# A one-core decoder step in split fp32: how a norm's squares are summed, where the last pair's low weight is made, who issues the sample rows, and a root written with one product less

## The chip, the cores and the metric

The program runs on one core of one Trainium2 chip. The metric is device time in microseconds (us) of one execution, the median of several runs. Five engines work side by side and wait for each other by semaphores: TensorE (PE in the profile; PEld is its weight load), VectorE (DVE), ScalarE (ACT), GpSimd (POOL) and SyncE (SP), which here only issues DMAs. Every engine takes its instructions in the order in which the program lists them.

## The reference

One layer of a hybrid decoder, for a prompt of 512 tokens and eight samples of four tokens each (544 columns in all), all in float32. With the names of the reference:

```
h = RMSNorm_pre(x);  [x_r | q | k | v | g] = h @ W_in
m = (sigmoid(g_A) * (lru(x_r) @ W_A) + sigmoid(g_B) * (attn(q,k,v) @ W_B)) @ W_out
x = x + RMSNorm_post(m)
u = RMSNorm_pre2(x) @ W_up ; u = causal depthwise conv (width 3) over positions
x = x + RMSNorm_post2((gelu(u_gate) * u_val) @ W_down)
```

where an RMSNorm is

```
y = x32 * lax.rsqrt(jnp.mean(x32 * x32, axis=-1, keepdims=True) + EPS) * g
```

The new rows of x and the recurrent, window and convolution states are the outputs. The width of x is 1024, of the feed-forward part 4096 (8192 columns up, gate and value).

## The kernel before

**Layout.** Activations lie transposed: 128 features on the partitions, tokens along the free axis. A [1024, 544] activation is eight chunks; a chunk is worked on in two halves of tokens, of 272 columns each after the mixer. A float32 product is made of three fast ones: each weight and each operand is split into a high part (a copy in the fast format, by ScalarE) and a low part (raw minus high, by VectorE), and TensorE adds high times high, high times low and low times high. A "product" in this text is 12 such matmuls: four 128-row chunks by three. The weight tiles `wh_...` and `wl_...` are the high and low parts. TensorE's order is written by hand, and so is the order of ScalarE, VectorE and GpSimd around the changes; the raw weights are loaded by SyncE several units ahead into five rotating buffers.

**The norm between mixer and feed-forward** (`norm_chain`, from L1233) runs once for each half of the tokens, as a generator whose pieces are slipped between TensorE's products. For the second half (a = 1) it does this, two chunks to a group g: VectorE scales the mixer's output (`mt`, L1258); the residual is added to give `x1` (names `x_0` to `x_7` in the trace), for even chunks on GpSimd (L1260) and for odd ones on VectorE (L1262); ScalarE squares each chunk into `sq_x` (L1266), chunk 0 straight into the sum `accx`. The other seven squares have to be added into `accx`. Two of these additions are done by DMAs that GpSimd issues (L1270): the squares of chunks 2 and 3 are accumulated into that of chunk 1, in memory, one DMA after the other since both write the same tile. VectorE adds 4, 5, 6, the collected chunk 1, and 7 (L1273). TensorE then sums over the partitions (`pst_f`), ScalarE and VectorE make the reciprocal root (`nst_f`) and a diagonal (`dg_f`), TensorE spreads it (`rep_f`), and VectorE writes the normed second half (`h2t`, split into `b12H` and so on).

Meanwhile TensorE works through early products on the first half: `pq` of columns 0, 32, 1, 33, 2, 34, 3, 35, each in two halves of the weight rows (`wh_e_0` or `wh_e_1`, split at L1465 on ScalarE, and `wl_e` at L168 on VectorE). ScalarE's and VectorE's instructions for these weights stand in the same queues as those of the norm.

**The feed-forward part** goes over 32 pairs (gate and value columns). A pair's up-projection, three-tap convolution (`tap`: the first on ScalarE, L1559; the other two on VectorE, tile `uc`), gelu, product `z` and split (`fH`, `fL`) are spread over later slots by `later(k, ...)`: k slots from now. `slot(k, lag)` closes a slot: it emits what is due in it, then the weights ahead (`consumed`, `ahead`: high parts by `do_high`, low parts lag units behind by `do_low`). Products with W_down (`pmdn`) go into three rotating PSUM banks (`PM`, L134), and VectorE adds each into `ft` (L1717, helper L174). For the last pair, 31, the chain is written out at L1683 to L1688.

**The end** (from L1925): tokens 256 to 511 and the sample rows go out transposed (`yo`, copied by ScalarE at L1811, issued by SyncE at L1812); of tokens 128 to 255 the two halves `xtok` are scaled by the reciprocal root `r` (L1895) and issued at L1896. The root is ScalarE's square root, a reciprocal, and one Newton step on VectorE (L1940 to L1944), all on 128x1 tiles `nst_t`.

Of the kernel before, what the change touches and what calls it, by code (L numbers as in the profile page):

```python
# [14 lines left out]
ALU = mybir.AluOpType  # L15
AX = mybir.AxisListType

P = 128
D = 1024
# [104 lines left out]
def hawk_step(ctx, tc, I, O):  # L124
    nc = tc.nc
# [47 lines left out]
    def add(out, a, b):  # L173
        dve.tensor_tensor(out=out, in0=a, in1=b, op=ALU.add)  # L174
# [1058 lines left out]
    def norm_chain(a, acc):  # L1233
# [8 lines left out]
        with tc.high_priority(offset=HP):  # L1242
            rep = spread(dg, n, f"m{a}")
            acc2 = T(f"accx{a}")
            sq = {}

            def x1_(c):
                return x1[c][:, lo:hi]

            for c in range(0 if a else 8):  # L1250
                m_ = mt[c][:, lo:hi]
                stt(m_, m_, pv[:, G_POST + c:G_POST + c + 1], rep[:, :n], ALU.mult, ALU.mult)
                pool.tensor_tensor(out=x1_(c), in0=x1_(c), in1=m_, op=ALU.add)
                sq_sum(acc2, x1_(c), n, c == 0, f"x{a}_{c}")
            for g in range(6 if a else 0):
                for c in range(2 * g, 2 * g + 2) if g < 4 else ():
                    m_ = mt[c][:, lo:hi]
                    stt(m_, m_, pv[:, G_POST + c:G_POST + c + 1], rep[:, :n], ALU.mult, ALU.mult)  # L1258
                    if c % 2 == 0:
                        pool.tensor_tensor(out=x1_(c), in0=x1_(c), in1=m_, op=ALU.add)  # L1260
                if g < 4:
                    add(x1_(c), x1_(c), m_)  # L1262
                for c in range(2 * g - 3, 2 * g - 1) if 1 <= g < 6 else ():
                    if 0 <= c < 8:
                        sq[c] = acc2 if c == 0 else T(f"sq_x{a}_{c}")
                        act.activation(sq[c][:, :n], x1_(c), AF.Square)  # L1266
                        if c == 0 and n % P:
                            pool.memset(acc2[:, n:n + P - n % P], 0.0)
                        if c in (2, 3):
                            pool.dma_start(out=sq[1][:, :n], in_=sq[c][:, :n], accum_op=ALU.add)  # L1270
                for c in ((), (), (), (), (4,), (5, 6, 1, 7))[g]:
                    if c:
                        add(acc2[:, :n], acc2[:, :n], sq[c][:, :n])  # L1273
                yield 0.5
        yield NORM_TICKS[a]
        with tc.high_priority(offset=HP):
# [364 lines left out]
    def pair(p_, nm):  # L1641

        jv, jg = p_, 32 + p_
        ps, e = pst.setdefault(p_, {}), e_.setdefault(p_, {})
        bank = {"a11": "x", "a12": "z", "p2": "x", "p3": "y", "p1": "x", "p4": "w" if p_ in apart else "x",
                "a22": "y"}[nm]
        start = bank not in ps
        if start:
            ps[bank] = PX(f"pu{bank}_{p_}")
        product(ps[bank], usplit["s", p_, nm], XOF[nm], start, nm in ("a12", "p4", "a22") or bank == "x" and nm == "p1" and p_ in apart)  # L1650
        z = ps[bank][:, :HN]

        def taken(nm_):

            e[nm_] = EP(f"{nm_}_{p_}")
            act.copy(e[nm_], z)  # L1656

        def u4_c22():
            taken("u4")
            ug = utile(jg)  # L1660
            for o, y in zip(halves2(ug, ps["y"]), halves2(ug, e["u4"])):
                sub(o[0], o[1], y[1])

        def c11():
            add(utile(jv)[:, 2:2 + HN], e["e1"], z)

        def c12():
            if p_ in apart:
                for o, y in zip(halves2(ut[jv], z), halves2(ut[jv], e["u4"])):
                    add(o[0], y[1], o[1])  # L1670
            else:
                for o in halves2(ut[jv], z):
                    act.copy(*o)
            states(jg if p_ < 31 else jv)

        def c21():
            sub(ut[jg][:, 2:2 + HN], z, e["u2"])
            states(jv if p_ < 31 else jg)

        if nm in ("a11", "a12", "p2", "p1", "p4", "a22"):  # L1680
            f = {"a11": lambda: taken("e1"), "a12": c11, "p2": lambda: taken("u2"), "p1": u4_c22, "p4": c12, "a22": c21}[nm]
            result(f)
        if p_ == 31 and nm in ("a22", "p4"):  # L1683
            j = jg if nm == "a22" else jv
            chain = [(1, tap, j, 0), (1, tap, j, 1), (2, tap, j, 2)]
            chain += [(2, glu, p_, 0)] if j == jg else [(2, glu, p_, 1), (3, glu, p_, 2), (3, glu, p_, 3)]
            for k, f, *args in chain:
                later(k, f, *args)  # L1688
        elif nm == "a22":
            for k, f, *args in ((1, tap, jv, 0), (2, tap, jv, 1), (2, tap, jg, 0), (3, tap, jv, 2), (4, tap, jg, 1),  # L1690
                                (5, tap, jg, 2), (6, glu, p_, 0), (7, glu, p_, 1), (8, glu, p_, 2), (9, glu, p_, 3)):
                later(k + 3 if k >= 8 and p_ % CH == CH - 1 else k, f, *args)
# [77 lines left out]
    for i, x in enumerate(plan):  # L1770
        more[0] = min(4, max(0, i - len(plan) + LASTS))
        if x[0] == "s":
            pair(*x[1:])
            slot()
        elif x[0] == "q":
            plain(*x)
            slot(x[3])
        else:
            _, q, c, a = x
            down(q, c, a, down_done(q, c))  # L1780
            slot(a)
        if i == len(plan) - 8:
            start_at(now[0] + 1, x1_again())
            start_at(now[0] + 3, ffn_states())
# [18 lines left out]
    def rows_t(i):  # L1803
        t0, nn, _ = TOK[i]
        dst = yp[t0:t0 + nn, :] if i < 4 else ys
        o = RAW(f"yo{i}")
        for kk in range(2):
            px = PX(f"pyo{i}_{kk}")
            for j in range(4):
                pe.transpose(px[:nn, j * P:(j + 1) * P], ft[4 * kk + j][:, t0:t0 + nn], ident)  # L1810
            act.copy(o[:nn, kk * 512:(kk + 1) * 512], px[:nn, :])  # L1811
        return lambda: nc.sync.dma_start(out=dst, in_=o[:nn, :])  # L1812

    sq7 = T("sq7")
    frow, fgs = {}, {}
# [108 lines left out]
        tokens_out(0, r0, z)()  # L1924
    order_.enter_context(tc.manual_schedule(engines={nc.sync.engine}))  # L1925
    fgs[1, 1] = T("fg1_1")[:, 0:512]
    st = SM("nst_t1", [P, 4], "nst_t")
    v, r, s_, b_ = (st[:, z:z + 1] for z in range(4))
    yo = [rows_t(2)]
    o = ends(0)  # L1930
    ends_square(0, o)
    ends_gain(0, o)
    add(b_, ssq[:, 1, 0:1], ssq[:, 1, 1:2])
    dve.tensor_scalar(b_, b_, 1.0 / D, EPS, ALU.mult, ALU.add)
    o = ends(1)
    ends_square(1, o)
    act.activation(s_, ssq[:, 1, 2:3], AF.Sqrt, scale=1.0 / D, bias=b_)
    ends_gain(1, o)
    yo += [rows_t(i) for i in (3, 4)]
    stt(v, ssq[:, 1, 2:3], 1.0 / D, b_, ALU.mult, ALU.add)  # L1940
    dve.reciprocal(r, s_)
    mul(s_, r, r)
    stt(s_, s_, -0.5, v, ALU.mult, ALU.mult)
    stt(r, s_, 1.5, r, ALU.add, ALU.mult)  # L1944
    xo = [tokens_out(1, r, z) for z in range(2)]
    for f in yo[:2] + xo[:1] + yo[2:] + xo[1:]:
        f()
    flush()
    order_.close()
# [32 lines left out]
```

## Time and profile before

| | |
|---|---|
| median of 3 runs | 997.18 us (996.15, 997.18, 998.26) |
| the profiled execution's own time | 998.1 us |
| its span, from first to last instruction | 996.3 us |
| mean granted clock of TensorE | 0.993 |
| PE busy | 985.0 us (99%) |
| DVE busy | 745.5 us (75%) |
| ACT busy | 557.8 us (56%) |
| POOL busy | 162.1 us (16%) |

The 1.8 us between 996.3 and 998.1 lie outside the recorded span. In the profile a row of the timeline gives start and length in us, the engine, the line of the program, the operation with output and inputs, the shape, how many instructions are merged ("x2"), and in brackets how long the engine had been idle before and what released it. A row of the waits gives waiter, its line, releaser, total us, times, longest. A row of a table by windows gives the stretch, its length, the busy time of PE, PEld, DVE, ACT (and POOL) with the number of instructions, TensorE's granted clock (1.00 is full speed), the DMA engines' busy share and GB/s.

### The profile page before, as it was taken

Reading aid. Unit: us, or ns where it says so; the run is one execution under the profiler, and the core shown is the slowest. Engines: PE = TensorE matmul, PEld = TensorE weight load, DVE = VectorE, ACT = ScalarE, POOL = GpSimd, SP = SyncE. Lnnn points to the kernel's source line nnn. Section 1 sums busy time; section 2 is a strip of 40 time slices with the busy share of each in tenths; the row PEclk is TensorE's granted clock in tenths of the full one; section 3 lists DMA queues with packets and bytes.
Section 4 is the critical chain, followed back from the end, with each engine's and each line's share of the span. In section 5 each row is a group of like instructions: output and inputs, shape, how many; then the busy total and the mean of one; then the engine's idle time right before and its main releaser. Section 6 shows DMA issues by size and latency. Waiting matters only on the chain.

```text
span 996.3 us, 20129 instructions
## 1 busy us (share of the span) xinstructions
PE 985.0 (99%) x7780; PEld 976.5 (98%) x7780; DVE 745.5 (75%) x1608; ACT 557.8 (56%) x1356; POOL 162.1 (16%) x273
## 2 busy tenths in 40 slices
PE   9999999999999999989999999999999999999997
PEld 8999999999999999989999999999999999999996
DVE  6677678767858555678787788888888888888765
ACT  6545334468476425545776655555655555556652
POOL 2162000002406341210001010101010101011004
PEclk9999999999999999998999999999999999999999
DMA  7674222333223535135147767676767677768612
GB/s 209 198 246 146 86 64 86 107 97 95 87 70 99 175 112 171 44 120 171 48 117 155 164 150 168 152 167 152 167 152 167 153 165 154 164 151 199 196 46 90
DMA packets 211399, 135.90 MB, mean 136 GB/s; under 512 B 8997, under 2 KB 197421, under 8 KB 211272
## 3 DMA queue, kind: packets, MB, share of 16 engines
q1 hardware_dynamic: 199032, 112.72, 39.6%
q0 software_dynamic: 12208, 19.87, 11.9%
q10 hardware_dynamic: 64, 2.04, 0.6%
q8 instruction: 61, 1.00, 0.4%
q14 instruction: 34, 0.28, 0.1%
HBM read 111.78 MB, written 11.37 MB: 124 GB/s over the span
## 4 chain that ended last, share of the span: by engine, by line
PE 96%; ACT 1%; DVE 1%; issue 1%; POOL 0%; DMA 0%; DVEq 0%; ACTq 0%; POOLq 0%
PE pmin L165 22%; PE pmdn L165 17%; PE pux L1528 16%; PE puy L1528 8%; PE pq L1528 7%; PE pmout L165 5%; PE pmao L165 5%; PE pmlo L165 5%; PE puz L1528 4%; PE pg L165 1%; PE psc L165 1%; PE pvp L165 1%; PE ptok L165 1%; PE pt L819 1%; PE ps_warm L165 0%
## 5 line engine op out<-in xcount | busy, mean ns | idle before, releaser
L165 PE MATMUL pmin<-hH,wh_in 128*128 128x256 f32 (+1 forms) x568 | 164.7, 292 | 0.0
L165 PE MATMUL pmin<-hL,wh_in 128*128 128x256 f32 (+1 forms) x568 | 162.3, 288 | 0.0
L165 PE MATMUL pmin<-hH,wl_in 128*128 128x256 f32 (+1 forms) x568 | 159.0, 288 | 0.0
L165 PE MATMUL pmdn<-fH,wh_dn 128*128 128x256 f32 (+1 forms) x448 | 129.3, 289 | 0.2 <-DVE ft L174 0.2
L165 PE MATMUL pmdn<-fH,wl_dn 128*128 128x256 f32 (+1 forms) x448 | 129.2, 288 | 0.0
L165 PE MATMUL pmdn<-fL,wh_dn 128*128 128x256 f32 (+1 forms) x448 | 128.8, 287 | 0.0
L177 DVE SCALAR_TENSOR_TENSOR uc<-u,fv,uc 128x560 f32<-128x560 f32 x128 | 101.9, 796 | 13.3 <-ACT uc L1559 13.2
L165 PEld LDWEIGHTS pmin<-hH,wh_in 128*128 128x128 f32 x568 | 107.2, 189 | 1.5 <-issue 1.2
L165 PEld LDWEIGHTS pmin<-hL,wh_in 128*128 128x128 f32 x568 | 107.3, 189 | 0.1
L165 PEld LDWEIGHTS pmin<-hH,wl_in 128*128 128x128 f32 x568 | 104.7, 188 | 0.2 <-issue 0.2
L165 PEld LDWEIGHTS pmdn<-fH,wh_dn 128*128 128x128 f32 x448 | 84.3, 188 | 0.6 <-issue 0.6
L165 PEld LDWEIGHTS pmdn<-fL,wh_dn 128*128 128x128 f32 x448 | 84.4, 188 | 0.0
L165 PEld LDWEIGHTS pmdn<-fH,wl_dn 128*128 128x128 f32 x448 | 84.4, 188 | 0.0
L1656 ACT COPY u<-pux 128x272 f32<-128x272 f32 x52 | 20.1, 386 | 86.3 <-PE pux L1528 86.3
L168 DVE TENSOR_TENSOR u<-puy,u 128x240 f32<-128x240 f32 (+2 forms) x78 | 24.6, 344 | 50.2 <-PE puy L1528 33.2
L283 ACT ACTIVATE wh_in<-raw_in 128x512 fp32r<-128x512 f32 x70 | 42.8, 627 | 31.6 <-issue 17.8
L174 DVE TENSOR_TENSOR ft<-ft,pmdn 128x256 f32<-128x256 f32 (+1 forms) x104 | 45.1, 435 | 17.2 <-PE pmdn L165 16.9
L290 DVE TENSOR_TENSOR wl_in<-raw_in,wh_in 128x512 fp32r<-128x512 f32 x70 | 48.0, 696 | 1.0 <-ACT wh_in L283 1.0
L1559 ACT ACTIVATE uc<-u,fv 128x560 f32<-128x560 f32 x64 | 48.3, 756 | 0.0
L1454 POOL DMA_DIRECT2D raw_up_s<-raw_up_s x26 | 22.4, 863 | 100.3 <-DMA raw_up_s<-raw_up__7493 4.9
L168 DVE TENSOR_TENSOR wl_dn<-raw_dn,wh_dn 128x512 fp32r<-128x512 f32 x56 | 38.3, 683 | 0.0
L776 ACT ACTIVATE s<-s,st 128x256 f32<-128x256 f32 (+1 forms) x32 | 15.2, 475 | 40.7 <-DVE st L773 23.1
(777 smaller groups left out, 3413.3 us busy)
## 6 DMA issues: line engine op xcount, KB each, us to landing
raw_in<-in_w_in_dram SPq DMA_DIRECT2D x35, 512.0 KB
raw_dn<-in_w_down_dram SPq DMA_DIRECT2D x56, 256.0 KB
raw_up_s<-in_w_up_dram SPq DMA_DIRECT2D x25, 512.0 KB
raw_up_s<-raw_up_s POOLq DMA_DIRECT2D x26, 256.0 KB, 5.2
raw_ao<-in_w_attn_o_dram SPq DMA_DIRECT2D x8, 512.0 KB
raw_lo<-in_w_lru_o_dram SPq DMA_DIRECT2D x8, 512.0 KB
raw_out<-in_w_out_dram SPq DMA_DIRECT2D x8, 512.0 KB
xdram<-xn POOLq DMA_DIRECT2D x8, 272.0 KB, 11.4
```

Of the source, the lines that this page charges most:

```text
L165: pe.matmul(out, l, r, start=start, stop=stop)
L168: dve.tensor_tensor(out=out, in0=a, in1=b, op=ALU.subtract)
L174: dve.tensor_tensor(out=out, in0=a, in1=b, op=ALU.add)
L177: dve.scalar_tensor_tensor(out=out, in0=a, scalar=s_, in1=b, op0=op0, op1=op1)
L283: act.activation(hl[0], raw, AF.Copy)
L290: (eng or dve).tensor_tensor(out=hl[1], in0=raw, in1=f32(hl[0]), op=ALU.subtract)
L776: act.activation(s3[:, j, :], s3[:, j, :], AF.Exp, bias=ng[:, j:j + 1], accum_out=sm[:, j:j + 1])
L819: pe.transpose(pt[:, (2 * ch + j) * P:(2 * ch + j + 1) * P], s3[:, j, ch * P:(ch + 1) * P], ident)
L1454: pool.dma_start(out=w["p4"], in_=w["p2"], accum_op=ALU.add)
L1528: pe.matmul(ps[:, :HN], w, x, start=start and k == 0 and i == 0, stop=stop and k == 3 and i == 2, skip_group_check=True)
L1559: act.activation(yt[j][:, 0:FLATU], u[:, 0:FLATU], AF.Copy, scale=fv[:, j:j + 1])
L1656: act.copy(e[nm_], z)
```

## The change

Four edits, which touch different places.

1. In the second half's norm, the two accumulating DMAs of GpSimd are gone. VectorE adds all seven squares, in two blocks: 1, 2, 3 in group 4, and 4, 5, 6, 7 in group 5.
2. In the last pair, the second tap of the value column moves one slot later, and the slot that closes the pair makes its low weight part with lag 0 instead of 1.
3. The sample rows' output DMA is issued by ScalarE's queue instead of SyncE's.
4. In the last root, minus one half of the mean square is prepared before the last sum arrives (`h_`), and `r * r * v` is one instruction in place of two. The tile is one column wider and has buffers of its own.

```diff
@@ norm_chain
                         act.activation(sq[c][:, :n], x1_(c), AF.Square)
                         if c == 0 and n % P:
                             pool.memset(acc2[:, n:n + P - n % P], 0.0)
-                        if c in (2, 3):
-                            pool.dma_start(out=sq[1][:, :n], in_=sq[c][:, :n], accum_op=ALU.add)
-                for c in ((), (), (), (), (4,), (5, 6, 1, 7))[g]:
-                    if c:
-                        add(acc2[:, :n], acc2[:, :n], sq[c][:, :n])
+                for c in ((), (), (), (), (1, 2, 3), (4, 5, 6, 7))[g]:
+                    add(acc2[:, :n], acc2[:, :n], sq[c][:, :n])
                 yield 0.5
@@ pair
-            chain = [(1, tap, j, 0), (1, tap, j, 1), (2, tap, j, 2)]
+            chain = [(1, tap, j, 0), (1 if j == jg else 2, tap, j, 1), (2, tap, j, 2)]
@@ the loop over the plan
             pair(*x[1:])
-            slot()
+            slot(1, int(x[1:] != (31, ENDS[-1])))
@@ rows_t
-        return lambda: nc.sync.dma_start(out=dst, in_=o[:nn, :])
+        return lambda q=nc.sync: q.dma_start(out=dst, in_=o[:nn, :])
@@ the end
-    st = SM("nst_t1", [P, 4], "nst_t")
-    v, r, s_, b_ = (st[:, z:z + 1] for z in range(4))
+    st = SM("nst_t1", [P, 5], "nst_t1")
+    v, r, s_, b_, h_ = (st[:, z:z + 1] for z in range(5))
...
     dve.tensor_scalar(b_, b_, 1.0 / D, EPS, ALU.mult, ALU.add)
+    dve.tensor_scalar(h_, b_, -0.5, 0.0, ALU.mult, ALU.add)
...
-    stt(v, ssq[:, 1, 2:3], 1.0 / D, b_, ALU.mult, ALU.add)
+    stt(v, ssq[:, 1, 2:3], -0.5 / D, h_, ALU.mult, ALU.add)
     dve.reciprocal(r, s_)
-    mul(s_, r, r)
-    stt(s_, s_, -0.5, v, ALU.mult, ALU.mult)
+    stt(s_, r, r, v, ALU.mult, ALU.mult)
     stt(r, s_, 1.5, r, ALU.add, ALU.mult)
     xo = [tokens_out(1, r, z) for z in range(2)]
-    for f in yo[:2] + xo[:1] + yo[2:] + xo[1:]:
+    yo[2](act)
+    for f in yo[:2] + xo:
         f()
```

TensorE's order is the same in both programs. The three places below are where the other engines' orders differ.

On GpSimd, in the second half's norm (`x_0` to `x_6` are the even residual chunks, `mt` the scaled mixer output, `sq_x_1` the tile that collects squares):

```order
 L1260 TENSOR_TENSOR x_0_4621<-x_0_4621,mt_5223 128x272
 L1260 TENSOR_TENSOR x_2_4623<-x_2_4623,mt_5225 128x272
-L1270 DMA sq_x_1_6016<-sq_x_2_6018 128x272
 L1260 TENSOR_TENSOR x_4_4625<-x_4_4625,mt_5227 128x272
-L1270 DMA sq_x_1_6016<-sq_x_3_6044 128x272
 L1260 TENSOR_TENSOR x_6_4627<-x_6_4627,mt_5229 128x272
```

The two accumulating DMAs no longer stand ahead of the additions for chunks 4 and 6. On VectorE, at the same place, before (`wl_e_0` and `wl_e_1` are low parts of early weights, `accx` the sum of squares):

```order
L168 TENSOR_TENSOR wl_e_0_6050<-raw_up__5711,wh_e_0_6049 128x512
L174 TENSOR_TENSOR accx_5963<-accx_5963,sq_x_4_6047 128x272
L168 TENSOR_TENSOR wl_e_1_6073<-raw_up__5709,wh_e_1_6072 128x512
L174 TENSOR_TENSOR accx_5963<-accx_5963,sq_x_5_6065 128x272
L174 TENSOR_TENSOR accx_5963<-accx_5963,sq_x_6_6067 128x272
L174 TENSOR_TENSOR accx_5963<-accx_5963,sq_x_1_6016 128x272
L174 TENSOR_TENSOR accx_5963<-accx_5963,sq_x_7_6090 128x272
L168 TENSOR_TENSOR wl_e_1_6097<-raw_up__5711,wh_e_1_6096 128x512
```

and with the change:

```order
L168 TENSOR_TENSOR wl_e_0_6048<-raw_up__5711,wh_e_0_6047 128x512
L174 TENSOR_TENSOR accx_5963<-accx_5963,sq_x_1_6016 128x272
L174 TENSOR_TENSOR accx_5963<-accx_5963,sq_x_2_6018 128x272
L174 TENSOR_TENSOR accx_5963<-accx_5963,sq_x_3_6043 128x272
L168 TENSOR_TENSOR wl_e_1_6073<-raw_up__5709,wh_e_1_6072 128x512
L174 TENSOR_TENSOR accx_5963<-accx_5963,sq_x_4_6045 128x272
L174 TENSOR_TENSOR accx_5963<-accx_5963,sq_x_5_6063 128x272
L174 TENSOR_TENSOR accx_5963<-accx_5963,sq_x_6_6065 128x272
L174 TENSOR_TENSOR accx_5963<-accx_5963,sq_x_7_6090 128x272
L168 TENSOR_TENSOR wl_e_1_6097<-raw_up__5711,wh_e_1_6096 128x512
```

Ahead of the first `wl_e_1` stand three additions where there was one, and between the two `wl_e_1` four as before. On VectorE in the last pair, before (`wl_dn` are low parts of W_down's weights, `uc` the taps, `z` the gated product, `ft` the sum over products, `fL` the low part of the last feed-forward chunk):

```order
L168 TENSOR_TENSOR wl_dn_6_12998<-raw_dn_6_12736,wh_dn_6_12997 128x512
L177 SCALAR_TENSOR_TENSOR uc_13054<-u_12889,fv,uc_13054 128x560
L174 TENSOR_TENSOR ft_7362<-ft_7362,pmdn_4_0_13036 128x256
L177 SCALAR_TENSOR_TENSOR uc_13054<-u_12889,fv,uc_13054 128x560
L177 SCALAR_TENSOR_TENSOR z_13072<-uc_13054,fv,uc_12994 128x512
L177 SCALAR_TENSOR_TENSOR z_13072<-uc_13054,fv,uc_12994 128x32
L168 TENSOR_TENSOR wl_dn_7_13017<-raw_dn_7_12778,wh_dn_7_13016 128x512
L174 TENSOR_TENSOR ft_7362<-ft_7362,pmdn_4_1_13057 128x288
L168 TENSOR_TENSOR fL_13094<-z_13072,fH_13093 128x544
```

and with the change:

```order
L168 TENSOR_TENSOR wl_dn_6_12998<-raw_dn_6_12736,wh_dn_6_12997 128x512
L168 TENSOR_TENSOR wl_dn_7_13017<-raw_dn_7_12778,wh_dn_7_13016 128x512
L174 TENSOR_TENSOR ft_7362<-ft_7362,pmdn_4_0_13037 128x256
L177 SCALAR_TENSOR_TENSOR uc_13055<-u_12889,fv,uc_13055 128x560 x2
L177 SCALAR_TENSOR_TENSOR z_13073<-uc_13055,fv,uc_12994 128x512
L177 SCALAR_TENSOR_TENSOR z_13073<-uc_13055,fv,uc_12994 128x32
L174 TENSOR_TENSOR ft_7362<-ft_7362,pmdn_4_1_13057 128x288
L168 TENSOR_TENSOR fL_13094<-z_13073,fH_13093 128x544
```

The low part `wl_dn_7` and the addition of `pmdn_4_0` now stand ahead of both taps.

## The prediction

> **What bounds the kernel now.** I read the page's busy times first, then the waits of TensorE, then the timelines around them.
>
> ```profile
> PE 985.0 (99%) x7780; PEld 976.5 (98%) x7780; DVE 745.5 (75%) x1608; ACT 557.8 (56%) x1356; POOL 162.1 (16%) x273
> ...
> PE pq L1528 <- ACT wh_e L1465: 2.8, 1, 2.8
> ```
>
> TensorE is busy nearly all the time, and the change leaves its instructions and their order alone. So time can only come from its pauses, from its clock, and from the tail after its last matmul. One pause stands out. Its chain, from GpSimd over ScalarE to TensorE, in the timeline:
>
> ```profile
> 438.18 0.94 POOL L1270 DMA_DIRECT2D sq_x<-sq_x  x1 [0.77 <-ACT sq_x L1266]
> 444.47 0.89 POOL L1270 DMA_DIRECT2D sq_x<-sq_x  x1 [4.54 <-issue]
> 445.11 1.04 POOL L1260 TENSOR_TENSOR x<-x,mt 128x272 f32<-128x272 f32 x1
> ...
> 446.18 0.43 ACT L1266 ACTIVATE sq_x<-x 128x272 f32<-128x272 f32 x1 [4.94 <-POOL x L1260]
> 446.51 0.61 ACT L1465 ACTIVATE wh_e<-raw_up__5709 128x512 fp32r<-128x512 f32 x1
> ...
> 444.12 0.28 PE L1528 MATMUL pq<-b11H,wl_e 128*128 128x272 f32 x1
> 447.18 0.59 PE L1528 MATMUL pq<-b21H,wh_e 128*128 128x272 f32 x1 [2.78 <-ACT wh_e L1465]
> ```
>
> Both accumulating DMAs write the same tile, so GpSimd holds the second until the first, issued at 438.18, has landed: it issues at 444.47. The addition for chunk 6 stands behind it and starts at 445.11. ScalarE's square of chunk 6 waits 4.94 us for that, and behind the square stands the high weight part that TensorE needs next. That is the 2.78 us.
>
> The pause costs more than its length. The windows of the granted clock (columns: window, length, busy PE, PEld, DVE, ACT, POOL, then the clock) and the matmul starts:
>
> ```profile
> 446.75:447.00 0.25, 0.00 (x0) 0.00 (x0) 0.00 (x0) 0.25 (x1) 0.00 (x0) 0.63 0.13 35
> 457.00:457.25 0.25, 0.25 (x3) 0.25 (x2) 0.00 (x0) 0.00 (x0) 0.00 (x0) 0.89 1.19 328
> ...
> 435.23 0.28 PE L1528 MATMUL pq<-b11H,wh_e 128*128 128x272 f32 x1
> ...
> 457.06 0.62 PE L165 MATMUL rep_f<-dg_f,ones 128*128 128x272 f32 x2
> ...
> 429.19 0.29 PE L1528 MATMUL pq<-b11H,wl_e 128*128 128x272 f32 x1
> 430.35 0.29 PE L1528 MATMUL pq<-b11L,wh_e 128*128 128x272 f32 x1
> ```
>
> A mean of 0.63 between 1 and one half puts the fall at about 446.82; 0.89 puts the return at about 457.05. So TensorE ran at half clock for 10.2 us.
>
> **Edit 1, the squares.** At full clock the six products from 435.23 to 444.12 (71 steps between 72 starts) took 0.125 us a matmul. A column sum of the kind of `pst_f` takes 0.91 more: the two starts at 429.19 and 430.35 have `pst_m` and one matmul between them, 1.16 less two steps. From the last matmul before the pause to `rep_f` stand three products and `pst_f`. At full clock `rep_f` would start at 444.12 + 0.125 + 36 x 0.125 + 0.91 = 449.66; it started at 457.06. The stretch is worth **7.40 us**: 2.93 of pause from the step to the next start, 4.47 of slow clock.
>
> What is left of it depends on whether everything is ready in time without the DMAs:
>
> ```profile
> 439.17 1.07 DVE L174 TENSOR_TENSOR x<-x,mt 128x272 f32<-128x272 f32 x1
> 440.76 0.89 DVE L177 SCALAR_TENSOR_TENSOR mt<-mt,pv,rep_m 128x272 f32<-128x272 f32 x2
> 441.69 0.44 DVE L174 TENSOR_TENSOR x<-x,mt 128x272 f32<-128x272 f32 x1
> 442.05 0.68 DVE L168 TENSOR_TENSOR wl_e<-raw_up__5711,wh_e 128x512 fp32r<-128x512 f32 x1
> 442.65 0.43 DVE L174 TENSOR_TENSOR accx<-accx,sq_x 128x272 f32<-128x272 f32 x1
> 447.16 0.69 DVE L168 TENSOR_TENSOR wl_e<-raw_up__5709,wh_e 128x512 fp32r<-128x512 f32 x1 [4.07 <-ACT wh_e L1465]
> ...
> 451.94 0.16 DVE L419 TENSOR_SCALAR nst_f<-pst_f 128x3 f32<-128x3 f32 x1 [0.44 <-ACT nst_f L418]
> 453.30 0.62 DVE L1166 TENSOR_SCALAR dg_f<-ident,nst_f 128x128 f32<-128x128 f32 x3
> ```
>
> GpSimd: `mt` of chunk 6 is ready at about 441.2 (half of the pair at 440.76), the addition takes 1.04 and ends near 442.3. ScalarE: the square takes 0.33 (446.18 to 446.51), the high weight part 0.61, done near 443.3. VectorE: from 442.65 three additions where one stood, 0.36 each (the step from 441.69 to 442.05), then the low part of 0.60 (442.05 to 442.65), done at about 444.4. TensorE reaches the product at 444.25 and needs this low part at its third matmul, 444.5. Then four additions to 445.9, and `pst_f` is reached at 445.75. Then three low parts (1.8) to 447.6, the root and one more low part (451.94 to 453.30: 1.36) and the diagonal (0.62), ready at 449.6, against `rep_f` at 449.66. Everything arrives within 0.2 us of its need. I take 0.2 us of new waits: **-7.2 us**. Bounds: -7.4 (no wait), and -5.4 if the waits add up to 2 us without the clock falling (it took 2.4 us from the last matmul's step at 444.25 to the fall). The two additions that VectorE gains (0.72 us) lie in the 4.07 us in which it sat idle before. SyncE's queue, where the write of x1's chunk 6 waits for the same addition, goes on earlier too, and TensorE waits for no load in this stretch.
>
> The page "TensorE: Matmul & The Clock Gate" of the Trainium skill, "Why this matters for your kernels", speaks against so large a term: it asks for no idle gaps over about 3 us, and this gap was shorter. By its Part 1, one busy window of 3.4 us also gives full speed back, a third of the 10.2 us seen. By that the term would be about -4.4 us; the trace of this execution does not agree.
>
> **Edit 2, the last pair.**
>
> ```profile
> 946.18 0.80 DVE L177 SCALAR_TENSOR_TENSOR uc<-u,fv,uc 128x560 f32<-128x560 f32 x1 [2.20 <-ACT uc L1559]
> 946.89 0.41 DVE L174 TENSOR_TENSOR ft<-ft,pmdn 128x256 f32<-128x256 f32 x1
> 948.89 0.68 DVE L168 TENSOR_TENSOR wl_dn<-raw_dn,wh_dn 128x512 fp32r<-128x512 f32 x1
> 951.70 0.45 DVE L174 TENSOR_TENSOR ft<-ft,pmdn 128x288 f32<-128x288 f32 x1
> ...
> 949.01 0.66 ACT L1578 ACTIVATE fH<-z 128x544 fp32r<-128x544 f32 x1 [2.34 <-DVE z L177]
> ...
> 946.98 0.29 PE L165 MATMUL pmdn<-fH,wl_dn 128*128 128x288 f32 x1
> 947.46 0.37 PE L165 MATMUL pmdn<-fH,wh_dn 128*128 128x288 f32 x1 [0.18 <-DVE ft L174]
> ...
> 951.62 0.29 PE L165 MATMUL pmdn<-fH,wl_dn 128*128 128x288 f32 x1
> 952.29 0.37 PE L165 MATMUL pmdn<-fH,wh_dl 128*128 128x288 f32 x1 [0.37 <-ACT ffn_rows_s L1747]
> ```
>
> With three PSUM banks a product waits until VectorE has added the one three before it. The product at 947.46 follows the addition at 946.89; that at 952.29 follows the addition at 951.70 (ending 952.15; the releaser named is another). Against a step of 0.13 they are late by 0.35 and 0.54 us. With the change the addition at 946.89 moves into VectorE's 2.20 us of idle time, and the first lateness goes. But the second decides, and it hangs on the taps, whose start at 946.18 waits for ScalarE as before. From there: two dependent taps of 0.82, `z` 0.83, ending near 948.75 where it ended at 948.98; `fH` starts 0.23 earlier, ends at 949.44; `fL` starts then instead of at 949.85. The low parts and additions behind it move up by 0.4. So **-0.4 us**; bounds 0 (`fL`'s successors wait for ScalarE's high parts) and -0.9 (both).
>
> **Edits 3 and 4, the tail.**
>
> ```profile
> 988.89 0.42 DVE L171 TENSOR_TENSOR fg<-pend,gpost 128x256 f32<-128x256 f32 x1 [0.80 <-ACT jke L1888]
> 989.49 0.16 DVE L171 TENSOR_TENSOR nst_t<-nst_t 128x1 f32<-128x1 f32 x1
> 990.14 1.42 DVE L177 SCALAR_TENSOR_TENSOR xtok<-fg,nst_t,xtok 128x512 f32<-128x512 f32 x2
> ...
> 990.92 0.33 SPq L1896 DMA_DIRECT2D out_dram<-xtok  x1
> 991.34 0.47 SPq L1812 DMA_DIRECT2D out_dram<-yo  x1
> 991.90 0.55 SPq L1896 DMA_DIRECT2D out_dram<-xtok  x1
> ...
> 993.25:993.50 0.25, 0.00 (x0) 0.00 (x0) 0.00 (x0) 0.00 (x0) 0.00 (x0) 0.50 1.83 246
> 993.50:993.75 0.25, 0.00 (x0) 0.00 (x0) 0.00 (x0) 0.00 (x0) 0.00 (x0) 0.50 0.22 49
> ```
>
> The instruction that goes is the 0.19 between 989.49 and the next start (989.68); the added one falls into the 0.80 us that VectorE idles ahead of the second half, and it waits for nothing new. So `xtok` starts at 989.95 and its second half ends at 991.37 instead of 991.56. SyncE's last issue stood at 991.90, behind the sample rows' at 991.34 with 0.47 of length; with those gone it follows its data, at 991.45: 0.45 earlier, 0.19 of it from the root. ScalarE's own issue waits for its last copy, and nothing is queued behind it. What the DMA engines then make of it, the two windows bound (last columns: clock, busy share, GB/s): a share of 1.83 at 246 GB/s and then a hole of 49 GB/s, before the last transfer's data. From 0 (the engines are full and only the order changes) to -0.95 (the 0.45 and a hole and slow spot of 0.5); I take **-0.5 us**, nearer to the earlier issue, since an engine with a hole isn't full.
>
> "DMA: Bandwidth & Descriptors" of the Trainium skill, "Issuing engines are not separate DMA queues", says that DMAs from any engine run on the same 16 engines and a second issuer saves only the time to initiate them. By that the transfer itself gains nothing, and edits 3 and 4 give the 0.45 of issue or less.
>
> **The sum.** -7.2 - 0.4 - 0.5 = -8.1 us. On the profiled execution's 998.1 us (span 996.3 and 1.8 around it) this gives 990.0. The median of the runs, 997.18, lies 0.9 lower; less 8.1 that is 989.1. I take the middle, **989.5 us**: the part that can differ between executions of the program before is the slow clock, which the program after should not have. Without rivals its range is 988 to 991.
>
> **Rivals.**
>
> *A. The clock didn't fall in the runs as it did in the profile.* The fall came 0.36 us before the pause ended (446.82 against 447.18), so it was a near thing; an execution in which it stays away has only the 2.93 to win. Then -2.9 + 0.2 - 0.4 - 0.5 = -3.6 on the median: 993.6. Against it: the three runs lie at 996.15 to 998.26 around the profile's 998.1, and none shows 4.47 less. The Trainium skill's "TensorE: Matmul & The Clock Gate", Part 1, has the activity window free-running, which would make such a difference between executions possible. Chance 0.08.
>
> *B. The pause only changes its name.* VectorE now carries three additions ahead of the low part; if that low part or the sum before `pst_f` is 2.4 us late, the clock falls again, and 2.4 + 4.47 of the 7.40 come back. Then -0.5 - 0.4 - 0.5 = -1.4: 995.8 to 996.7. For it: my slack is 0.2 us. Against it: it needs twelve times that. Chance 0.05.
>
> *C. Slower, by additions at the contended price.* The addition at 439.17 took 1.07, not 0.44, while GpSimd was adding too. If all seven paid this, each is 0.71 later than its 0.36: 2.1 ahead of the low part and 2.8 more ahead of `pst_f`. That is 5.0 us of pauses and, at a loss of 4.47 for 10.2 us of half clock, 4.5 to 6 more of slow clock if it falls at each of the two: about 11 in place of 7.4, so +3.6 - 0.9 = +2.7, 999.9. It decides from about 4 us of pauses with such a clock. Against it: GpSimd's last addition ends near 442.3, ahead of the first of VectorE's. Chance 0.04.
>
> **The numbers.** Forecast 0.83, A 0.08, B 0.05, C 0.04. About 0.2% (2 us) is what a measurement of this kernel can tell from no change. Faster by more: the forecast and A, 0.91. Within: B, 0.05. Slower: C, 0.04. The range takes the forecast's own, the smaller term of edit 1 (-5.4 gives 991.3) and the best ends (-7.4, -0.9, -0.95 give 988.9 on the profile, 987.9 on the median): 987.5 to 992.0. A, B and C lie outside.
>
> **What would show it.** In the profile after: no waits of `pq` on `wh_e`, a granted clock of 1.00 between 444 and 458, `rep_f` near 449.7 to 450.0, and GpSimd's chunk 6 near 441.3. In the last pair, the product at 947.46 starts at 947.1, and the one at 952.29 at 951.9 (both less 7.2), still with a wait. In the tail, SyncE's last issue 0.1 us behind the last `xtok`. The prediction is wrong if TensorE still waits over 2 us near `pst_f`, for then the clock goes with it; or if the clock falls without such a wait.

## The result and the profile after

| | before | with the change |
|---|---|---|
| median | 997.15 us (6 runs, 995.06 to 998.85) | 990.89 us (6 runs, 990.71 to 991.52) |
| ratio, with its 95% interval | | 0.9939 (0.9926 to 0.9951) |
| the profiled execution: time, span, mean granted clock | 998.1, 996.3, 0.993 | 991.07, 989.3, 0.998 |

The kernel is faster by 6.3 us; the forecast was 989.5, with 987.5 to 992.0 around it. The two spans differ by 7.0 us. Where they went is read by cutting both spans at four points that both kernels have: the start of the `pq` product near 435 us, the first `pq` matmul on the second half (`b12H`), the last `pend` matmul and the end. First the kernel before, then the changed one, from the timeline of TensorE (start, length, instruction; the first cut of the kernel before, 435.23, stands in the prediction):

```profile
462.84 0.37 PE L1528 MATMUL pq<-b12H,wh_e 128*128 128x272 f32 x1
987.99 0.28 PE L1884 MATMUL pend<-wl_dl,fH 128*128 128x256 f32 x1
```

```profile
435.12 0.28 PE L1525 MATMUL pq<-b11H,wh_e 128*128 128x272 f32 x1
455.91 0.37 PE L1525 MATMUL pq<-b12H,wh_e 128*128 128x272 f32 x1
980.74 0.28 PE L1881 MATMUL pend<-wl_dl,fH 128*128 128x256 f32 x1
```

| stage | before | with the change | difference |
|---|---|---|---|
| start to the first cut | 435.23 | 435.12 | -0.11 |
| norm stretch (edit 1) | 27.61 | 20.79 | -6.82 |
| feed-forward part (edit 2) | 525.15 | 524.83 | -0.32 |
| tail (edits 3 and 4) | 8.31 | 8.56 | +0.25 |

Edit 1 brought nearly everything, edit 2 about what was forecast, and edits 3 and 4 nothing.

**The norm stretch after.** All waits of TensorE, from the view of the waits of the changed kernel (waiter, its line, releaser, total us, times, longest):

```profile
PE pm_first L165 <- DVE wh_in L285: 1.1, 1, 1.1
PE ps_warm L165 <- POOL ones L219: 1.0, 1, 1.0
PE pmdn L165 <- DVE ft L174: 0.6, 1, 0.6
PE pst_f L165 <- DVE accx L174: 0.3, 1, 0.3
```

The wait of `pq` on `wh_e` is gone. The timelines of GpSimd, ScalarE, VectorE and TensorE show the chain that had made it, and what is left:

```profile
440.85 0.78 POOL L1260 TENSOR_TENSOR x<-x,mt 128x272 f32<-128x272 f32 x1 [1.39 <-DVE mt L177]
441.67 0.43 ACT L1266 ACTIVATE sq_x<-x 128x272 f32<-128x272 f32 x1 [0.90 <-POOL x L1260]
442.00 0.62 ACT L1462 ACTIVATE wh_e<-raw_up__5709 128x512 fp32r<-128x512 f32 x1
442.46 1.38 DVE L174 TENSOR_TENSOR accx<-accx,sq_x 128x272 f32<-128x272 f32 x3
443.76 0.68 DVE L168 TENSOR_TENSOR wl_e<-raw_up__5709,wh_e 128x512 fp32r<-128x512 f32 x1
444.36 1.94 DVE L174 TENSOR_TENSOR accx<-accx,sq_x 128x272 f32<-128x272 f32 x4
444.13 0.28 PE L1525 MATMUL pq<-b21H,wh_e 128*128 128x272 f32 x1
444.50 0.39 PE L1525 MATMUL pq<-b21H,wl_e 128*128 128x272 f32 x1
446.35 0.83 PE L165 MATMUL pst_f<-ones,accx 128*128 128x1 f32 x6 [0.34 <-DVE accx L174]
450.14 0.63 PE L165 MATMUL rep_f<-dg_f,ones 128*128 128x272 f32 x2
```

GpSimd adds chunk 6 at 440.85, where it had started at 445.11. `wh_e` starts at 442.00, ready well ahead of the product that starts at 444.13 without a wait. But VectorE's additions take 0.43 us a step in the block of three (442.46 to 443.76) and 0.48 in the block of four (1.94), where the sum had 0.36. So the low part of 443.76 ends at 444.44, and the matmul that reads it, the third of its product, starts at 444.50 where two steps of 0.125 after 444.13 would be 444.38. The sum of squares is late too, and `pst_f` waits 0.34. The price was to be seen before: there the four additions stood as one block,

```profile
447.77 1.94 DVE L174 TENSOR_TENSOR accx<-accx,sq_x 128x272 f32<-128x272 f32 x4
```

which is 0.48 each, while the sum took its 0.36 from an addition followed by a low part. The granted clock in windows (window, length, busy PE, PEld, DVE, ACT, POOL, then clock, DMA share and GB/s), first before, then with the change:

```profile
447.00:450.00 3.00, 2.82 (x11) 2.59 (x12) 2.67 (x6) 2.57 (x7) 0.00 (x0) 0.50 1.01 326
450.00:457.00 7.00, 7.00 (x33) 7.00 (x32) 3.97 (x13) 1.97 (x5) 0.00 (x0) 0.50 0.87 254
```

```profile
447.00:450.00 3.00, 3.00 (x25) 3.00 (x25) 2.90 (x12) 1.98 (x5) 0.00 (x0) 1.00 0.84 250
450.00:454.00 4.00, 4.00 (x33) 3.92 (x32) 3.71 (x9) 1.32 (x2) 0.00 (x0) 1.00 0.89 247
```

With the change TensorE starts 25 instructions between 447 and 450 where it started 11 (read the count behind its busy time), and 33 in 4 us where 33 took 7: full clock against half.

**The last pair and the tail after.** From the timelines of TensorE, VectorE and SyncE:

```profile
945.04 0.38 PE L165 MATMUL pmdn<-fH,wh_dl 128*128 128x288 f32 x1 [0.63 <-DVE ft L174]
982.25 0.41 DVE L177 SCALAR_TENSOR_TENSOR nst_t<-nst_t 128x1 f32<-128x1 f32 x2
982.75 1.41 DVE L177 SCALAR_TENSOR_TENSOR xtok<-fg,nst_t,xtok 128x512 f32<-128x512 f32 x2
983.53 1.04 SPq L1893 DMA_DIRECT2D out_dram<-xtok  x2
983.87 0.36 ACTq L1809 DMA_DIRECT2D out_dram<-yo  x1
```

One of the two waits of the last pair is gone, the other is now put down to `ft` (0.63). In the tail the issues did what was forecast: SyncE's last one ends at 984.57, 3.83 us after the last `pend` matmul started, where in before it ended at 992.45, 4.46 after. Yet the end comes no earlier.

### The profile page after: what moved, and what is told of

It reads as the page before. It is cut to its first block, busy times and chain, and to the rows that moved or that the text cites. A ratio compares the mean times of both kernels' runs of the same rounds, so it can differ in the third digit from the quotient of the medians.

```text
span 989.3 us, 20126 instructions
## 1 busy us (share of the span) xinstructions
PE 979.6 (99%) x7780; PEld 971.6 (98%) x7780; DVE 746.8 (75%) x1610; ACT 558.3 (56%) x1356; POOL 160.9 (16%) x271
## 4 chain that ended last, share of the span: by engine, by line
PE 96%; DVE 2%; ACT 1%; issue 0%; DVEq 0%; POOL 0%; ACTq 0%; POOLq 0%
PE pmin L165 22%; PE pmdn L165 17%; PE pux L1525 16%; PE puy L1525 8%; PE pq L1525 6%; PE pmout L165 5%; PE pmao L165 5%; PE pmlo L165 5%; PE puz L1525 4%; PE pg L165 1%; PE psc L165 1%; PE pvp L165 1%; PE ptok L165 1%; PE pt L819 1%; PE ps_warm L165 0%
```

## The experiments

Each kernel ran beside the kernel before on the same chip. The times are medians, with the lowest and highest in brackets.

### Edit 1 alone, and edits 2 to 4 alone

The first is the kernel before with the diff of `norm_chain`, the second the changed kernel with that diff undone.

> The kernel before with edit 1 alone (the two accumulating DMAs gone, VectorE adds all seven squares). Theory: the whole gain is the pause of TensorE and the slow clock behind it, and the other three edits cancel out: rep_f at about 450.1, median 991.0 to 991.5, as with the whole change (990.89). Rival: the other edits carry a visible share: median 991.8 or more.

> The change without edit 1 (edits 2, 3 and 4 on the kernel before). Theory: the pause at 444 and the half clock stay; the last pair gives 0.3 us, the root 0.15, the tail takes 0.3 to 0.4 back; the median lies within 0.6 us of the kernel before in the same session and its runs scatter by 2 to 4 us as those do. Rival: a median 1 us or more below it, or runs as close together as those of the whole change (0.8 us).

Measured: edit 1 alone 991.25 us (5 runs, 991.05 to 991.61), ratio 0.9953 (0.9939 to 0.9966); edits 2 to 4 alone 997.04 (11 runs, 994.16 to 999.44), ratio 1.0003 (0.9991 to 1.0016). The kernel before in these runs: 996.57 (21 runs, 994.53 to 999.03). By the same four cuts the norm stretch is 20.79 with edit 1 alone, the feed-forward part 524.83 with edits 2 to 4 against 525.18 without them, and the tail 8.39 with them against 8.31 without.

Edits 2 to 4 together can't be told from nothing in the times, since these scatter by 5 us. The profile of that kernel shows one thing that can differ between executions. Its pause in the timeline of TensorE, and its granted clock in windows:

```profile
446.45 0.39 PE L1528 MATMUL pq<-b21H,wh_e 128*128 128x272 f32 x1 [2.37 <-ACT wh_e L1465]
455.51 0.62 PE L165 MATMUL rep_f<-dg_f,ones 128*128 128x272 f32 x2
```

```profile
444.00:448.00 4.00, 1.42 (x9) 1.12 (x9) 1.50 (x4) 2.55 (x7) 1.42 (x2) 1.00 0.68 179
448.00:448.25 0.25, 0.25 (x4) 0.25 (x3) 0.25 (x1) 0.25 (x2) 0.00 (x0) 0.85 0.89 246
448.25:454.75 6.50, 6.49 (x29) 6.17 (x28) 4.89 (x15) 2.58 (x7) 0.00 (x0) 0.50 0.89 260
455.00:458.00 3.00, 3.00 (x24) 2.92 (x24) 1.76 (x5) 0.67 (x2) 0.00 (x0) 1.00 0.94 259
```

The same accumulating DMAs, nearly the same pause; but here the clock falls at 448.18, 1.7 us after the product has begun, and is back at 455.0: 6.8 us of half clock, where the profile of before had 10.2.

### The pause kept, TensorE kept busy

The kernel before, with ten matmuls of the tile of ones by itself (each shown as two instructions) ahead of the waiting product; nobody reads them.

```diff
+                if (z, u) == (4, 1) and j == early[4]:
+                    busy = PM("busy")
+                    for _ in range(10):
+                        mm(busy[:, :P], ones, ones, True, True)
                 plain("e", j, u, 0)
```

> The kernel before, with ten matmuls of ones that nobody reads put on TensorE ahead of the product that waits (about 2.5 of the 2.9 us of pause). Theory: the pause stays, the clock doesn't fall: the product starts at about 447.2 as before, rep_f at about 452.7 instead of 457.06, the time falls by about 4.4 to some 993 to 994, and the runs lie within 1 us. Rival: the slow stretch has nothing to do with the pause, or the early stretch is not what separates the runs: time 997 as before, spread 3 us.

Measured: 994.40 us (11 runs, 994.10 to 995.17), ratio 0.9987 (0.9978 to 0.9995). The timeline of TensorE and the windows:

```profile
444.17 2.39 PE L165 MATMUL busy<-ones 128*128 128x128 f32 x20
446.84 0.39 PE L1528 MATMUL pq<-b21H,wh_e 128*128 128x272 f32 x1 [0.28 <-ACT wh_e L1465]
453.22 0.62 PE L165 MATMUL rep_f<-dg_f,ones 128*128 128x272 f32 x2
```

```profile
447.00:450.00 3.00, 2.46 (x18) 2.02 (x18) 2.83 (x7) 2.24 (x6) 0.00 (x0) 1.00 0.99 312
450.00:457.00 7.00, 7.00 (x56) 6.92 (x56) 6.60 (x19) 3.30 (x7) 0.00 (x0) 1.00 0.99 276
```

The product starts nearly as late as in before (11.68 us behind the first cut, against 11.95), and the clock stays at 1.00: it is the idleness of TensorE that costs it, not the load on the other engines. One profile would not show this, as in some executions the clock of before stays up too; but all eleven executions of this kernel have a mean granted clock of 0.998 to 1.000, and their scatter is 1.1 us. The executions of the kernel before (39 in the three sets of runs) go with their own mean granted clock at both ends: the six at 0.993 took 997.58 to 999.03 us, the five at 0.998 took 994.53 to 994.79, about as long as with TensorE kept busy. Between, the order is rough (the thirteen at 0.996 took 995.02 to 998.42), and one reason is that the mean also counts the half clock after the last matmuls, which costs no time: in the ten profiles whose norm stretch ran at 1.00 it is 0.998 to 1.000. So in some executions the clock hardly falls, if at all, and the profiled one of before was among those where it fell longest. The fall of 4.4 us that was expected is that of the profiled execution. On the medians the slow clock cost 996.57 - 994.40 = 2.2 us, and the pause itself 994.40 - 991.25 = 3.15.

### The sample rows back on SyncE

The changed kernel, with the order of issues of the kernel before.

```diff
-    yo[2](act)
-    for f in yo[:2] + xo:
+    for f in yo[:2] + xo[:1] + yo[2:] + xo[1:]:
```

> The change with edit 3 undone alone: the sample rows are issued by SyncE again, between the two halves of xtok. Theory: the rows in ScalarE's queue share the DMA engines with the last two transfers and stretch them, which cost 0.3 to 0.4 us from the start of xtok to the end of the span (6.55 us with the change, 6.16 before): median 990.4 to 990.7, xtok to end 6.2. Rival: the longer tail was chance of one execution and the earlier issue helps by up to 0.45: median 991.1 to 991.4, xtok to end 6.5 or more.

Measured: 990.95 us (5 runs, 990.83 to 991.47), ratio 0.9952 (0.9939 to 0.9964): the same as the changed kernel, and neither the time of the theory nor that of the rival. Its tail is 8.30 us. So edit 3 gained nothing and edit 4 next to nothing. The tails of all kernels that have the sample rows last: 8.31, 8.31 and 8.33 with edits 3 and 4 undone; 8.30 and 8.38 with edit 4 alone; 8.39, 8.56 and 8.38 with both. The last three are programs of one tail, so 0.2 us is what one profile can tell.

### Two of the additions on GpSimd

The changed kernel, with squares 2 and 3 added into that of chunk 1 by GpSimd (`pool` in the code). A second kernel of this pair had the sample rows on SyncE as well.

```diff
-                for c in ((), (), (), (), (1, 2, 3), (4, 5, 6, 7))[g]:
+                        if c in (2, 3):
+                            pool.tensor_tensor(out=sq[1][:, :n], in0=sq[1][:, :n], in1=sq[c][:, :n], op=ALU.add)
+                for c in ((), (), (), (), (4,), (5, 6, 1, 7))[g]:
```

> The kernel after, with one thing changed: the squares of chunks 2 and 3 are added into that of chunk 1 by two GpSimd additions (128x272, as its others, 0.78 each) in place of two of VectorE's seven; VectorE then adds 4, then behind the low part 5, 6, 1, 7. After still has a wait of 0.34 us at pst_f, which starts about 0.5 us later than my sum had it, because seven additions of 0.46 stand on VectorE where I took 0.36. Theory (what is left of edit 1's price is VectorE's additions): pst_f starts 0.3 to 0.5 earlier against the first product, no wait there, rep_f too, the time falls by 0.3 to 0.5: 990.4 to 990.6. Rival (GpSimd's additions cost it back): its addition for chunk 4 stands behind the second one of them and starts 0.7 later, and VectorE's additions beside GpSimd take 0.7; the wait moves to a weight part ahead of a product: 990.9 to 991.5. Both have the granted clock at 1.00 there, since no wait is over 1 us.

> The kernel after, with the two GpSimd additions of the run before and with the sample rows issued by SyncE between the two halves of xtok, as in the kernel before. If the two are independent, this is the run before within 0.2 us: 990.3 to 990.7, and yo's issue to the end takes 5.8 us in place of after's 6.04. Rival (the sample rows' place is worth nothing in either direction in the times): no difference that five rounds show. It is meant as a candidate for the best version.

Measured: 990.84 us (5 runs, 990.62 to 990.93) and 990.70 (5 runs, 990.64 to 991.62). The norm stretch is 20.73 and 20.72 against 20.79. From the timelines of GpSimd, VectorE and TensorE of the first:

```profile
437.63 1.85 POOL L1270 TENSOR_TENSOR sq_x<-sq_x,sq_x 128x272 f32<-128x272 f32 x2 [0.54 <-ACT sq_x L1266]
439.43 0.97 POOL L1260 TENSOR_TENSOR x<-x,mt 128x272 f32<-128x272 f32 x1
439.70 1.26 DVE L168 TENSOR_TENSOR wl_e<-raw_up__5709,wh_e 128x512 fp32r<-128x512 f32 x1
443.16 0.39 PE L1527 MATMUL pq<-b11H,wl_e 128*128 128x272 f32 x1 [0.35 <-DVE wl_e L168]
446.04 0.83 PE L165 MATMUL pst_f<-ones,accx 128*128 128x1 f32 x6
```

The rival's mechanism came true, at a smaller price than it had. `pst_f` no longer waits. But GpSimd's addition for chunk 4 comes later (439.43 here, 438.69 in the changed kernel), and VectorE's low part, which starts beside it, takes 1.26 us in place of 0.68. VectorE's later work slips, and another low part makes TensorE wait 0.35. The wait only changed its name.

### The sample rows left out

The changed kernel without that DMA, so the sample rows' output is not written; their transposes and copies stay.

```diff
-    yo[2](act)
     for f in yo[:2] + xo:
```

> The kernel after, without the output DMA of the sample rows (32 rows of 1024, 128 KB; that output is not written; their transposes and copies stay). Theory (in the tail the DMA engines are busy moving, and the sample rows beside the last halves stretch them; who issues them matters little): 128 KB less at the 250 to 340 GB/s of these windows is 0.4 to 0.5 us, so yo's issue to the end takes about 5.6 in place of 6.04, and the time is 990.4 to 990.6. Rival (the end is set by the last xtok's issue and a fixed latency behind it; the rows are hidden): 6.0, and 990.9.

Measured: 989.88 us (5 runs, 989.62 to 990.08), 1.0 below the changed kernel; the tail is 7.36 us. That is twice what the theory allowed for these 128 KB. The DMA engines in windows (the last two columns are their busy share and GB/s), with the rows (the changed kernel) and without:

```profile
983.80:985.05 1.25, 0.00 (x0) 0.00 (x0) 0.36 (x1) 0.04 (x1) 0.00 (x0) 1.00 1.00 400
985.05:986.55 1.50, 0.00 (x0) 0.00 (x0) 0.00 (x0) 0.00 (x0) 0.00 (x0) 0.56 1.02 266
986.55:987.30 0.75, 0.00 (x0) 0.00 (x0) 0.00 (x0) 0.00 (x0) 0.00 (x0) 0.50 0.82 300
```

```profile
983.55:986.05 2.50, 0.00 (x0) 0.00 (x0) 0.30 (x1) 0.00 (x0) 0.00 (x0) 1.00 0.99 390
986.05:986.30 0.25, 0.00 (x0) 0.00 (x0) 0.00 (x0) 0.00 (x0) 0.00 (x0) 1.00 0.25 82
```

Without the rows the engines move 390 GB/s to the last byte. With them they are as busy (a share of 1.02) and move 266: the rows are not only 128 KB more, they are slow.

### The same bytes from 128 partitions

The changed kernel, with the rows' DMA reading a quarter of the tile of tokens 384 to 511 (128 partitions of 256 numbers); that output holds other numbers.

```diff
+    rows128 = []
...
+        if i == 3:
+            rows128.append(o[:, 0:256])
+        if i == 4:
+            return lambda q=nc.sync: q.dma_start(out=ys.rearrange("t (a c) -> (t a) c", a=4), in_=rows128[0])
```

> The kernel after, with the sample rows' DMA at the same place and of the same 128 KB, but read from 128 partitions of 256 numbers each (the first quarter of the tile of tokens 384 to 511) in place of 32 partitions of 1024; so that output holds other numbers. Without the rows the end came 7.36 us after the last pend matmul starts, with them 8.3 to 8.6: 1.1 us for 128 KB, where the stream beside it moves 128 KB in 0.33 us (393 GB/s). Theory (it is the form of the transfer, 32 long rows from 32 partitions, which takes the engines about three times as long a byte): from 128 partitions it costs 0.3 to 0.4, so 7.7 to 7.8 after the last pend matmul, and 990.2 to 990.3. Rival (it is a second queue or one more transfer in flight, of any form, that stretches the end): 8.3 to 8.6 as in after, 990.9.

Measured: 990.50 us (4 runs, 990.15 to 990.82); the tail is 7.65, as the theory had it; the time is 0.2 above the theory's. This tile is ready earlier, and so the DMA was issued earlier, at 983.47, 2.1 us after the last `pend` matmul (3.1 in the changed kernel); part of the gain can be due to that. What the form costs the engines is free of it. The rows' queue in the table of DMA queues (packets, MB, share of 16 engines' time from 978 to 990 us), first the changed kernel, then this one, then the kernel of the next section, in which tokens 384 to 511 go by that queue (128 partitions of 1024 numbers, four times the bytes):

```profile
q10 hardware_dynamic: 48, 0.13, 6.0%
```

```profile
q10 hardware_dynamic: 144, 0.13, 3.2%
```

```profile
q10 hardware_dynamic: 144, 0.52, 11.0%
```

The same bytes take the engines half the time when they come from 128 partitions. The third line tells the number of partitions from the length of a row: with the same 4 KB a row as the sample rows, but from 128 partitions, 128 KB cost 11.0 / 4 = 2.75%. So it is the 32 partitions, not the long rows.

### The sample rows first

The changed kernel, with the sample rows transposed, copied and issued (by SyncE) ahead of tokens 384 to 511, which ScalarE's queue then issues. In a second kernel tokens 384 to 511 also went out in two halves, the first on SyncE.

```diff
-    yo += [rows_t(i) for i in (3, 4)]
+    yo += [rows_t(i) for i in (4, 3)]
```

> The kernel after, with the sample rows transposed, copied and issued ahead of tokens 384 to 511: SyncE issues tokens 256 to 383, the rows, the two halves of xtok; ScalarE's queue issues tokens 384 to 511 behind its last copy. The rows can then go into the hole that the DMA engines have between 983.05 and 983.55 in after. Theory (the rows cost the tail about 1.1 us because they come among the last transfers): the end 7.6 to 8.0 after the last pend matmul starts, against 8.3 to 8.6, and 990.2 to 990.6. Rival (512 KB of tokens 384 to 511 now come 1 us later and are the last transfer; the rows only change places): 8.3 or more, 990.9 to 991.5.

> As rows_first, but tokens 384 to 511 go out in two halves of 256 KB: the first is issued by SyncE when its copy ends, about 983.35, ahead of the halves of xtok, the second by ScalarE's queue behind the last copy. Theory (from 983.3 on the DMA engines then have something to move at every moment, and what has to be moved, 1.1 MB at 393 GB/s, sets the end): 7.4 to 7.8 after the last pend matmul, 990.0 to 990.4, at least as good as rows_first. Rival (one more issue on SyncE, 0.4 to 0.6 us, delays xtok's last half): not better than rows_first.

Measured: 990.55 us (5 runs, 990.26 to 990.64), ratio 0.9940 (0.9927 to 0.9953), tail 7.94; with halves 990.62 (5 runs, 990.52 to 990.86), tail 8.11. The DMA engines of the first, in windows:

```profile
983.80:984.55 0.75, 0.00 (x0) 0.00 (x0) 0.48 (x1) 0.15 (x1) 0.00 (x0) 1.00 0.80 183
984.55:987.05 2.50, 0.00 (x0) 0.00 (x0) 0.00 (x0) 0.00 (x0) 0.00 (x0) 0.84 1.02 397
```

The rows now go at 183 GB/s while nothing else is ready, and what follows runs at 397 to the end. Of the versions that compute everything this has the lowest median, 0.3 us below the changed kernel, and the shortest tail. Its runs all lie below those of the changed kernel (990.71 and up), but the two were not run side by side, and their ratios to the kernel before are alike (0.9940 and 0.9939); so the 0.3 us is read from the tail, not shown by the times. The halves brought no more, as the rival had it.

## Why the prediction was right, and where it was off

**Edit 1: the mechanism was right.** The two accumulating DMAs held GpSimd, GpSimd held ScalarE, ScalarE held TensorE, and the pause took the clock with it. Edit 1 alone takes the norm stretch from 27.61 to 20.79 (20.79 to 20.82 in all seven profiles with VectorE's seven additions), and TensorE kept busy in the same pause keeps its clock at 1.00.

**Its size in the profiled executions** was 6.82, not 7.2. The failed item is "three additions where one stood, 0.36 each": they took 0.43 to 0.48, as the block of four in the profile of before did, so the low part came late by 0.1 and `pst_f` started at 446.35 and not 445.75, and `rep_f` at 450.14 and not 449.66. Of the 7.40 that the stretch was worth, 0.58 us stayed where I took 0.2, inside the bounds: 0.34 is the wait of `pst_f`, and 0.23 was lost in the product before it, whose twelve starts from 444.13 to 445.73 take 1.60 us in place of 1.37. GpSimd's chunk 6 was no part of that: it came at 440.85 and took 0.78, where I had 441.2 and 1.04. One reading beside it was off: from 444.25 to the fall of the clock it is 2.57 us, and 2.4 only from that matmul's end.

**Its size on the median** was mis-sized by more: 5.3 us by edit 1 alone (996.57 to 991.25), 3.15 of pause and 2.2 of clock, where the sum had 4.47 of clock. The step at fault is pricing the slow clock by one execution and taking it off the median. Rival A was half true: in some executions the clock doesn't fall, and those (994.53 to 994.79) lie 3.6 to 3.9 above the changed kernel, where A had 3.6. That A's sum fits so well is in part luck: it had 2.7 for the pause and 0.9 for the other edits, and the runs show 3.15 and 0.3 to 0.4. Its error, and mine in arguing against it, was to treat it as true of all executions or none. The evidence against it was thin: three times within 2.1 us, when a kernel whose clock stays up scatters by about 1.

**The page on the clock.** "TensorE: Matmul & The Clock Gate" of the Trainium skill asks in "Why this matters for your kernels" for no gaps over about 3 us. The trace doesn't agree: the clock fell at gaps of 2.4 and 2.8 us, though not in all executions. Its Part 1 has a window of 3.4 us that runs freely: the two stretches of half clock, 6.8 and 10.2 us, are two and three of these. The record of the clock in the traces bears such steps out: in all twelve kernels, what lies between two changes of the clock is a whole multiple of 3.413 us (10.24 and 6.83 us of half clock, 979.63 or 983.04 where the clock stayed up). In the step that ended with the fall TensorE was idle for 2.4 us in before and 1.7 us with edits 2 to 4 alone, and the rest of the pause lay outside it. So a window whose place differs between executions would let the same gap cost nothing in one and 10 us of half clock in another. The Trainium skill's rule that one busy window gives full speed back isn't what these two profiles show: in both, the clock came back only after two whole steps without a pause (450.23 to 457.05, and 448.18 to 455.0). By that rule the term was -4.4 us, and I dismissed it by one execution; on the medians it was -5.3, nearer to it than to my -7.2. That the window's place decides was not tried, and no trace here is of an execution of before whose clock stayed up.

**Edit 2** brought 0.32 to 0.35 us in the stage (525.15 or 525.18 to 524.83), where 0.4 was forecast. The three profiles without it have 525.15 to 525.18, eight with it 524.77 to 524.89. The ninth, with the rows back on SyncE, has 525.52: there TensorE loses 0.7 us at a weight part near 900 us, 45 us ahead of the last pair. That is twice what edit 2 gains, so times that can hold such a wait hardly show it. The first of the two waits went, the second stayed, as argued: the product at 945.04 is 0.32 ahead of before's 952.29 less the 6.93 by which the second cut moved.

**Edits 3 and 4** failed: -0.5 was forecast, and the tail went from 8.31 to 8.4 or 8.6. The step that fell is "an engine with a hole isn't full". The earlier issue came as computed, but the share of 1.83 at 246 GB/s ahead of that hole was the rows' own slow transfer (its packets are the rows', of 4 KB, at 0.49 us each, where the tokens' packets of 4 KB take 0.16), and moving its issue to another queue left it among the last ones. "Issuing engines are not separate DMA queues" of the Trainium skill ("DMA: Bandwidth & Descriptors") had this right: the transfer gained nothing, and the time to initiate it, which it would let one save, was not on the path either.

**The sum.** Against its own profiled execution: 0.38 (edit 1), 0.08 (edit 2) and 0.75 (edits 3 and 4) less than forecast, and 0.11 gained ahead of the first cut: 1.1 us, from 990.0 to 991.07. The rest of the 1.4 us between 989.5 and 990.89 is the middle between profile and median, which carried half of before's 0.9 over to a kernel whose median lies only 0.2 below its profile. So all three terms and the choice of the middle erred the same way, toward more gain; the forecast held because its range was wide enough, not because errors cancelled. Rivals B and C didn't come: no wait over 0.34 us is left in the norm stretch.

One thing in the description of the kernel before was too strong: the order of GpSimd in the norm stretch isn't written by hand (L1756 fixes that of ScalarE and VectorE alone). The program's text has the addition for chunk 4 ahead of the first accumulating DMA and that for chunk 6 ahead of the second; the trace has each behind. In the order of the text, the addition for chunk 6 would not stand behind the second DMA, and the DMAs might have stayed without the pause. That was not tried.

## What to carry to other kernels

When TensorE is the bound, follow the chain behind its longest pause across all engines, and look at the granted clock behind it; but take its price from several executions' clocks, since one profile may show the worst of them. Filling a pause with matmuls that nobody reads is a cheap way to measure what the clock alone costs (2.2 us here) and what the wait itself does. In a tail, look at what moves slowly rather than at who issues it: a transfer at half rate costs the same from any queue, and goes where nothing else is ready to move.

## What the runs showed of the hardware that was not expected

- The clock can fall after the pause is over: in the profile of edits 2 to 4 alone it fell 1.7 us behind the restart of the product that had waited, and stayed at half for 6.8 us; in before, it fell 0.36 us ahead of the restart, for 10.2.
- 128 KB stored from 32 partitions of 4 KB took the DMA engines about twice the time of the same bytes from 128 partitions of 1 KB (6.0% against 3.2% in the queue's share; 2.75% from 128 partitions of 4 KB), and alone they moved at 183 GB/s over 0.75 us, where the other stores ran at 390 to 400. In the tail that cost 1.0 us.
- Beside an addition on GpSimd, VectorE's low part took 1.26 us in place of 0.68.
- Additions of 128x272 into the same sum took VectorE 0.43 to 0.48 us each in blocks of three and four, where one followed by a low part took 0.36.
